# Scan of a hybrid RWKV-7 encoder on one core: b and k in one load, values by heads and tokens, systems in longer rows

## The chip, the core and the metric

The kernel runs on one NeuronCore of a Trainium2 chip. The core has a matrix engine (TensorE, PE in the profile, with its weight loads as PEld), a vector engine (VectorE, DVE), a scalar engine (ScalarE, ACT), a general engine (GpSimd, POOL) and a sync engine (SyncE, SP). In this kernel SP issues nearly all transfers between DRAM and on-chip memory (SBUF); ACT issues a few from its own queue (ACTq). All transfers run on the same 16 DMA engines, as packets. Matmul results land in PSUM and are copied out by ACT or DVE. The metric is the device time of one execution in microseconds (us), lower is better.

## The reference

The reference is an encoder of two layers over 256 prompt tokens and 1024 sample tokens of 1024 features: a bidirectional RWKV-7 mixer, a neighbourhood attention, and an MLP after each. The change touches only the RWKV-7 mixer, whose core is a linear recurrence, run per head (16 heads of 64 features) forward and backward:

```
def _wkv_scan(r, w, k, v, a, b, reverse):
    def step(S, inp):
        r_t, w_t, k_t, v_t, a_t, b_t = inp
        sa = jnp.einsum('bhvk,bhk->bhv', S, a_t)
        S = S * w_t[:, :, None, :] + sa[..., None] * b_t[:, :, None, :] + v_t[..., None] * k_t[:, :, None, :]
        return S, jnp.einsum('bhvk,bhk->bhv', S, r_t)
    ...
    _, y = lax.scan(step, s0, seq, reverse=reverse)
    return jnp.moveaxis(y, 0, 1)
```

## The kernel before

**Stages.** The projections of the first layer come first (up to about 690 us of the profiled run), then the scan (to about 1365 us), then output projection, MLP, attention and second MLP. All arithmetic is float32, the large matmuls as three passes over split operands.

**The scan in chunks.** The 1280 tokens are 20 chunks of 64 (4 of the prompt, 16 of the sample). Inside a chunk the recurrence is solved in closed form: for each head, chunk and direction a triangular system of 64 x 64 has to be inverted, after which the state is handed on by matmuls. Two heads lie in the upper and lower 64 partitions of a tile, so every product is issued as a pair of 64-row matmuls (`pair`, L976). There are ten jobs of 16 chunks with two directions: jobs 0 and 1 take the prompt (four head pairs of four chunks each), jobs 2 to 9 the sample of one head pair each. A job has eight groups `(d, g)`: direction d, four chunks.

**What a job does.** The preparation stage has stored, per head pair and direction, `ar_d` (a in columns 0 to 63, r in 64 to 127) and `bk_d` (b in columns 0 to 63, k in 64 to 127), and `v_block` has stored the values into `v_d`. Then, for each job:

- `load` (L801, L802) brings a group's `ar` (128 partitions x 4 x 128) and `bb`, the b half of `bk_d` (128 x 4 x 64). `prod` multiplies them into `aps`; ACT copies the system half into `zb` (L814), DVE masks the other (L815). `store` (L818) writes the systems to a DRAM scratch `dd`, one for each direction, laid out `[16 chunks, 2 heads, 64, 64]`.
- `mload` (L833) reads the diagonal blocks of 32 x 32 back, so that each partition holds one block: direction 0 into `mt`, direction 1 into `mraw`, two transfers each. Four ACT copies `mtr` (L842) turn `mraw` into the second half of `mt`. DVE inverts all 128 blocks together in 31 rank-one steps (L853, L855).
- `qst` stores the inverse `q` and its transpose `qt` (L866, L870) to scratch `qd`; `qld` (L886, L891) loads them as `qq` and `qx`; `merge1` and `merge2` join the blocks of 32 into inverses of 64 (`yps`, `qps`).
- `kload` (L917) loads all of `bk_d` for the group (128 x 4 x 128), about 30 time units after the b half of the same rows was loaded; `kprod`, `kmask` and `ktr` make `kps`, `zk`, `lps` and `lt` of it.
- `vload` (L954) loads the values: `v_d` is `[tokens, 1024]`, so a partition (a token of the chunk) gets rows of 64 floats (256 bytes). Jobs 0 and 1 need 16 such transfers of 64 KB, the others 4 of 256 KB.
- `scan_step` runs 16 steps in each direction (16 time units): matmuls into `wu` and `yo`, with ACT copies `up` (L997), `u` (L1011) and `S` (L1019) between them. `scan_post` normalises and stores the result.

**What sets the order.** Every piece has a due time in units of a step, `at(t, f)`; sorted by due time, the pieces give PE, DVE, ACT and POOL an order written out by hand, in which each engine runs strictly. SP's order is not written out this way; it issues in order too. The systems of a job are prepared about 34 units (two jobs) ahead. Tiles of `ar`, `bb` and `zb` come from rings (`nxt`): `bb` has four slots and `ar` and `zb` 20 each, ten of them in the pool `er` that is opened during the value projection (`scan_begin`) and ten in `rp`, opened when the scan begins (`scan`). `bk` has three buffers. A load into a ring waits until the readers of the slot's last content are done.

**Around it.** `v_block` projects the values in 40 blocks of 128 tokens x 256 features (L510 to L512); ACT copies the result to `vt` (two buffers) and issues the store itself (L517). `gate_begin` loads the gate's operands during the last job through `graw`, of seven buffers.

Of the kernel before, what the change touches and what calls it, by code (L numbers as in the profile page):

```python
# [5 lines left out]
F32 = mybir.dt.float32  # L6
# [7 lines left out]
P = 128  # L14
T = 1280
# [3 lines left out]
L = 64  # L19
# [29 lines left out]
class Trunk:  # L49
# [50 lines left out]
    def l0_proj(self):  # L100
# [2 lines left out]
        r_d = self.dram("r_d", [2, P, T])  # L103
        vm_d = self.dram("vm_d", [8, P, T])
        sg_d = self.dram("sg_d", [160, T])
        v_d = self.dram("v_d", [T, 1024])
        pos = [1, 258, 770]
        W = 1283

# [296 lines left out]
        ev = {}  # L406
# [41 lines left out]
        def vmm(i):  # L448
            q, tb = i // 10, i % 10
            vw = [tuple(z[:, k % 2 * 256:k % 2 * 256 + 256] for z in wq["v", q, k // 2]) for k in range(KT)]  # L450
            ev[i] = self.v_block(act, vw, v_d, (vp, "vt", 256, 2), (self.pa, "aps"), q, tb, later=True)
        for i in range(40):
            at(vt(i), vmm, i)
            at(vt(i) + VL, lambda i=i: ev.pop(i)())
# [45 lines left out]
            self.v_split(vp, self.v_raw(w, vp, q, g), out, 8, str(q % 2), self.nc.vector)  # L500
        return out

    def v_block(self, act, vw, dst, tp, pp, q, tb, scale=1.0, later=False):

        nc = self.nc
        ps = pp[0].tile([P, 512], F32, name="vps", tag=pp[1])
        ts_ = slice(tb * P, (tb + 1) * P)
        for k in range(KT):
            ah, al = act[k]
            nc.tensor.matmul(ps[:, :256], ah[:, ts_], vw[k][0], start=k == 0, stop=False)  # L510
            nc.tensor.matmul(ps[:, :256], ah[:, ts_], vw[k][1], start=False, stop=False)  # L511
            nc.tensor.matmul(ps[:, :256], al[:, ts_], vw[k][0], start=False, stop=k == KT - 1)  # L512

        def evac():
            vt = tp[0].tile([P, tp[2]], F32, name="vt", tag=tp[1], bufs=tp[3])
            nc.scalar.activation(vt[:, :256], ps[:, :256], AF.Copy, scale=scale)
            nc.scalar.dma_start(dst[ts_, q * 256:(q + 1) * 256], vt[:, :256])  # L517
        if later:
            return evac
        evac()  # L520
# [183 lines left out]
    def scan_begin(self):  # L704

        nc, tc = self.nc, self.tc
        self.dram("z_d", [8, P, T])
        self.spool = lambda name, bufs, **kw: self.sctx.enter_context(tc.tile_pool(name=name, bufs=bufs, reuse_waits="tile", **kw))


        self.ectx = ExitStack()
        er = self.er = self.ectx.enter_context(tc.tile_pool(name="er", bufs=1, reuse_waits="tile", side="right"))
        self.r_bb, self.r_ar, self.r_zb = ([[er.tile([P, 4, w], F32, name=f"{name}{i}") for i in range(n)], 0] for name, n, w in
                                           (("bb", 4, L), ("ar", 10, P), ("zb", 10, P)))
        self.dsc = self.sctx.enter_context(tc.tile_pool(name="dsc", bufs=4, space=DRAM))
# [16 lines left out]
    def scan(self):  # L732
# [9 lines left out]
        self.lnx = fx.tile([P, 8, 2, L], F32, name="lnx")  # L742
        for e in range(2):
            nc.sync.dma_start(self.lnx[self.half(1 - e)], self.a["lnx"][:, :, 64 * e:64 * e + 64].unsqueeze(0).to_broadcast([64, 8, 2, L]))
        grow(self.r_ar, rp, "ar", [P, 4, P], 10)
        grow(self.r_zb, rp, "zb", [P, 4, P], 10)
        self.sp = pool("sp", 4)
        self.yp = pool("yp", 2)
        self.pa = self.pt = self.sctx.enter_context(tc.tile_pool(name="pa", bufs=4, space=PSUM, reuse_waits="tile"))
# [30 lines left out]
    def scan_job(self, j):  # L780
# [8 lines left out]
        T0 = -34.0  # L789

        def first(J=J):
            J["dd"] = [self.dsc.tile([16, 2, 64, 64], F32, name="dd", tag="dd") for _ in range(2)]
        at(T0, first, min(j + 1, 3))
        for n, (d, g) in enumerate(order):
            m, c0 = grp[g]
            t = T0 + 2 * n
            E = 1 if j == 0 else 2 if j == 1 and n < 2 else 3

            def load(d=d, g=g, m=m, c0=c0):
                ar, bb = self.nxt(self.r_ar), self.nxt(self.r_bb)  # L800
                nc.sync.dma_start(ar, self.ar_d[m, d, :, c0:c0 + 4, :])  # L801
                nc.sync.dma_start(bb, self.bk_d[m, d, :, c0:c0 + 4, 0:64])  # L802
                J["ar"][d, g], J["bb", d, g] = ar, bb

            def prod(c, d=d, g=g):
                ar, bb = J["ar"][d, g], J["bb", d, g]
                if c == 0:
                    J["zb"][d, g] = self.nxt(self.r_zb)
                    J["pa"] = self.pa.tile([P, 4, P], F32, name="aps", tag="aps")
                ps = J["pa"]  # L810
                if c < 4:
                    self.pair(lambda e, z: (ps[z, c, :], bb[z, c, :], ar[z, c, :]))
                if c == 4:
                    nc.scalar.copy(J["zb"][d, g][:, :, 0:64], ps[:, :, 0:64])  # L814
                    nc.vector.tensor_tensor(out=J["zb"][d, g][:, :, 64:128], in0=ps[:, :, 64:128], in1=self.mask[d][:, 64:128].unsqueeze(1).to_broadcast([P, 4, L]), op=ALU.mult)  # L815

            def store(d=d, g=g, j=j):
                nc.sync.dma_start(J["dd"][d].rearrange("c e s t -> (e s) c t")[:, 4 * g:4 * g + 4, :], J["zb"][d, g][:, :, 0:64])  # L818
            at(t - (1.614 if j else 7.0), load, E)
            for c in range(5):  # L820
                at(t + (c * 0.133 + -0.013 if c < 4 else 0.577), lambda c=c, f=prod: f(c), E)
            at(t + (1.263 if j else 1.011), store, E)
# [4 lines left out]
        def mload():  # L827
            mt = self.er.tile([P, 32, 32], F32, name="mt", tag="mt")
            raw = self.er.tile([P, 32, 32], F32, name="mraw", tag="mraw")
            for d in range(2):  # L830
                for b in range(2):
                    o, bs = 64 * d + 32 * b, slice(32 * b, 32 * b + 32)
                    nc.sync.dma_start((mt, raw)[d][o:o + 32], J["dd"][d].rearrange("c e s t -> (c e) s t")[:, bs, bs])  # L833
# [40 lines left out]
        def qld():  # L874
            Q = self.nxt(self.r_q)
            qx = [self.nxt(r) for r in self.r_qx]
            J["Q"], J["qx"] = Q, qx
            for d in range(2):
                hi = 32 - 32 * d
                nc.gpsimd.memset(Q[:, :, d, hi:hi + 32], 0.0)  # L880
            for d in range(2):
                for b in range(2):
                    o = 64 * d + 32 * b
                    for e in range(2):
                        q0 = 64 * e + 32 * b
                        nc.sync.dma_start(Q[q0:q0 + 32, :, d, 32 * b:32 * b + 32], J["qd"][d, o:o + 32].rearrange("(c e) s t -> e s c t", e=2)[e])  # L886

                o = 96 * d
                for e in range(2):
                    r0 = 64 * e + 32 * d  # L890
                    nc.sync.dma_start(qx[d][r0:r0 + 32], J["qd"][1 - d, o:o + 32].rearrange("(c e) s t -> e s c t", e=2)[e])  # L891
        at(T3 + 0.807, qld)

        for n, (d, g) in enumerate(order):
# [17 lines left out]
            at(t + 0.52, merge1)  # L912
            at(t + 1.30, merge2)

            def kload(d=d, g=g, m=m, c0=c0):
                bk = J["bk", d, g] = self.rp.tile([P, 4, P], F32, name="bk", tag="bk", bufs=3)
                nc.sync.dma_start(bk, self.bk_d[m, d, :, c0:c0 + 4, :])  # L917
# [12 lines left out]
            def ktr(c, d=d, g=g):  # L930
# [9 lines left out]
            at(t - 1.9, kload)  # L940
# [5 lines left out]
        def vload():  # L946
# [1 line left out]
            vd = self.scr["v_d"]  # L948
            parts = [(grp[0][0], grp[0][1], 0, 16)] if grp[0][1] else [(m, c0, 4 * g, 4) for g, (m, c0) in enumerate(grp)]
            for m, c0, k, n in parts:  # L950
                rows = slice(c0 * L, (c0 + n) * L)
                for i in range(2):
                    for e in range(2):
                        nc.sync.dma_start(vt[self.half(e ^ i), i, k:k + n], vd[rows, m * P + 64 * e:m * P + 64 * e + 64].rearrange("(c s) v -> s c v", s=L))  # L954
        at(-5.423, vload)

        def yalloc():
# [225 lines left out]
    def gate_begin(self):  # L1183
# [5 lines left out]
        def begin():  # L1189
# [6 lines left out]
            gp.tile([P, 512], F32, name="graw", tag="graw", bufs=7)  # L1196
            self.wo = []

        def load(src, c0, c1, stacked):
            raw = self.gp.tile([P, 512], F32, name="graw", tag="graw", bufs=7)  # L1200
            raw = raw[:, :c1 - c0]
            if stacked:
                for j in range(3):
# [696 lines left out]
```

## Time and profile before

| What | Value |
|---|---|
| median of 3 timed runs | 4072.04 us (4071.78 to 4072.08) |
| the profiled execution's own time | 4061.69 us |
| its span | 4059.9 us |
| PE busy | 3818.0 us (94%) |
| DVE busy | 2244.7 us (55%) |
| ACT busy | 1580.4 us (39%) |
| POOL busy | 1339.0 us (33%) |
| DMA packets | 450885, 394.89 MB; 267456 of them under 512 bytes |

The profile is that of one execution. Busy time counts compute instructions; issuing a transfer is listed by queue (SPq, ACTq). A row of the waits names an engine, the instruction that waited, what it waited for, then the total in us, how often, and the longest. A row of the timeline gives start, length, engine, line, operation, tiles, count, and in brackets the idle time before it and what ended it. "issue" is idle time of an engine that waited for nothing that the profile shows.

### The profile page before, as it was taken

The page shows a single profiled execution, that of the slowest core. Times are in us where ns is not written, and L with a number is a line of the kernel's source. Part 1 is how long each engine was busy: PE and PEld are TensorE (multiplying, and loading weights), DVE is VectorE, ACT ScalarE, POOL GpSimd, SP SyncE. Part 2 cuts the span into 40 slices and gives each one's busy share as a digit, 9 for nine tenths or more (in the row PEclk, how much of TensorE's full clock was granted, in tenths as well). Part 3 has the DMA queues.
Part 4 walks back from the last instruction along what each step waited for, and adds up shares of the span by engine and source line. Part 5 has one row for each costly group of instructions (what it writes and reads, how often), then busy time and mean ns, then how long its engine had stood idle before and what let it go on. Part 6 is the DMA issues. An engine that isn't in the chain of part 4 may idle for free.

```text
span 4059.9 us, 91014 instructions
## 1 busy us (share of the span) xinstructions
PE 3818.0 (94%) x36820; PEld 3225.7 (79%) x36820; DVE 2244.7 (55%) x4581; ACT 1580.4 (39%) x3868; POOL 1339.0 (33%) x1252
## 2 busy tenths in 40 slices
PE   8989988788888799999999999999989999999999
PEld 5765578787888688888888879887778888888888
DVE  5777742466565547555555562355554755555555
ACT  6776642455555431111111133466563211111111
POOL 4446542022122434222222241344443422222222
PEclk9987889899999899999999999999999999999999
DMA  4236564767664430111111115344464110111101
GB/s 142 71 102 223 194 216 121 163 159 169 157 158 122 131 113 32 42 38 36 42 37 37 42 51 168 113 111 108 94 181 150 40 41 33 42 37 37 42 32 63
DMA packets 450885, 394.89 MB, mean 97 GB/s; under 512 B 267456, under 2 KB 352832, under 8 KB 450464
## 3 DMA queue, kind: packets, MB, share of 16 engines
q1 hardware_dynamic: 416048, 327.72, 28.5%
q10 hardware_dynamic: 34416, 61.35, 4.2%
q8 instruction: 289, 4.73, 0.5%
q14 instruction: 132, 1.08, 0.1%
HBM read 270.50 MB, written 124.44 MB: 97 GB/s over the span
## 4 chain that ended last, share of the span: by engine, by line
PE 78%; DVE 6%; ACT 5%; DMA 4%; issue 3%; POOL 3%; SPq 1%; ACTq 0%; DVEq 0%; POOLq 0%
PE ps L95 19%; PE ps L96 18%; PE ps L97 18%; PE wu L976 4%; PE vps L510 1%; PE vps L512 1%; PE vps L511 1%; PE kps L976 1%; PE aps L976 1%; PE lps L976 1%; PE op L1815 1%; PE yo L976 1%; PE pt L1758 1%; PE yps L976 1%; DMA dd<-zb 1%
## 5 line engine op out<-in xcount | busy, mean ns | idle before, releaser
L1361 DVE TENSOR_TENSOR x<-ps,x 128x256 f32<-128x256 f32 x1488 | 814.1, 594 | 644.9 <-PE ps L97 644.8
L95 PE MATMUL ps<-ah,whi 128*128 128x512 f32 (+1 forms) x2304 | 842.4, 366 | 0.0
L96 PE MATMUL ps<-al,whi 128*128 128x512 f32 (+1 forms) x2304 | 825.8, 358 | 0.0
L97 PE MATMUL ps<-ah,wlo 128*128 128x512 f32 (+1 forms) x2304 | 823.1, 357 | 1.8 <-DVE wlo L90 1.5
L90 POOL TENSOR_TENSOR wlo<-raw,whi 128x1024 fp32r<-128x1024 f32 (+1 forms) x178 | 390.5, 2194 | 850.5 <-ACT whi L89 826.2
L95 PE MATMUL ps<-hh,whi 128*128 128x512 f32 (+1 forms) x1536 | 547.1, 356 | 9.4 <-DVE x L1361 9.4
L96 PE MATMUL ps<-hl,whi 128*128 128x512 f32 (+1 forms) x1536 | 546.3, 356 | 0.0
L97 PE MATMUL ps<-hh,wlo 128*128 128x512 f32 (+1 forms) x1536 | 545.8, 355 | 0.0
L95 PEld LDWEIGHTS ps<-ah,whi 128*128 128x128 f32 x2304 | 434.4, 189 | 72.2 <-issue 7.8
L97 PEld LDWEIGHTS ps<-ah,wlo 128*128 128x128 f32 x2304 | 433.4, 188 | 72.3 <-DVE wlo L90 1.9
L96 PEld LDWEIGHTS ps<-al,whi 128*128 128x128 f32 x2304 | 434.5, 189 | 62.5 <-issue 1.0
L89 ACT CAST whi<-raw 128x1024 fp32r<-128x1024 f32 (+1 forms) x206 | 200.3, 972 | 709.1 <-PE ps L96 624.9
L1340 POOL TENSOR_TENSOR rl<-rl 128x512 f32<-128x512 f32 (+1 forms) x192 | 173.7, 905 | 506.0 <-PE ps L97 462.5
L95 PEld LDWEIGHTS ps<-hh,whi 128*128 128x128 f32 x1536 | 291.2, 190 | 53.8 <-DVE x L1361 11.4
L97 PEld LDWEIGHTS ps<-hh,wlo 128*128 128x128 f32 x1536 | 291.4, 190 | 41.7
L96 PEld LDWEIGHTS ps<-hl,whi 128*128 128x128 f32 x1536 | 291.0, 189 | 40.7
L1339 ACT ACTIVATE rl<-ps 128x512 f32<-128x512 f32 (+1 forms) x192 | 100.7, 525 | 555.9 <-PE ps L97 555.9
L1342 ACT CAST hh<-rl 128x512 fp32r<-128x512 f32 (+1 forms) x192 | 105.6, 550 | 323.6 <-POOL rl L1340 323.6
L1343 DVE TENSOR_TENSOR hl<-rl,hh 128x512 fp32r<-128x512 f32 (+1 forms) x192 | 119.7, 624 | 143.1 <-ACT hh L1342 142.7
L1752 POOL TENSOR_TENSOR s<-s,mx 128x384 f32<-128x384 f32 (+1 forms) x150 | 109.7, 744 | 163.6 <-DVE mx L1751 115.4
L1057 POOL TENSOR_TENSOR y<-y,mu 128x512 f32<-128x512 f32 x18 | 19.3, 1073 | 370.4 <-DVE mu L1054 370.4
L853 DVE TENSOR_TENSOR tmp<-mt,q 128x31 f32<-128x31 f32 (+15 forms) x310 | 114.0, 368 | 43.3 <-ACT mt L842 20.3
(302 smaller groups left out, 8270.1 us busy)
## 6 DMA issues: line engine op xcount, KB each, us to landing
raw<-in_w_down_dram SPq DMA_DIRECT2D x64, 512.0 KB
raw<-in_w_up_dram SPq DMA_DIRECT2D x64, 512.0 KB
ar<-ar_d SPq DMA_DIRECT2D x80, 256.0 KB
bk<-bk_d SPq DMA_DIRECT2D x80, 256.0 KB
ar_d<-ar ACTq DMA_DIRECT2D x32, 512.0 KB
bk_d<-bk ACTq DMA_DIRECT2D x32, 512.0 KB
bs<-tab SPq DMA_DIRECT2D x128, 96.0 KB
v_d<-vt ACTq DMA_DIRECT2D x80, 128.0 KB
```

The costliest lines, as they stand in the source:

```text
L89: nc.scalar.copy(hi[:, cs], raw)
L90: lo_eng.tensor_tensor(out=lo[:, cs], in0=raw, in1=hi[:, cs].bitcast(F32), op=ALU.subtract)
L95: mm(ps, sh, mh, start=first, stop=False)
L96: mm(ps, sh, ml, start=False, stop=False)
L97: mm(ps, sl, mh, start=False, stop=last)
L853: nc.vector.tensor_tensor(out=tv, in0=mt[:, 0:jj, jj:jj + 1].to_broadcast([P, jj, w]), in1=q[:, jj:jj + 1, jj:].to_broadcast([P, jj, w]), ...
L976: self.nc.tensor.matmul(out, w, x, start=start, stop=stop, skip_group_check=free)
L1340: nc.gpsimd.tensor_tensor(out=r[:, :n], in0=r[:, :n], in1=r[:, :n], op=ALU.mult)
L1342: nc.scalar.copy(hh[:, :n], r[:, :n])
L1343: nc.vector.tensor_tensor(out=hl[:, :n], in0=r[:, :n], in1=hh[:, :n].bitcast(F32), op=ALU.subtract)
L1361: nc.vector.tensor_tensor(out=xv, in0=ps[:, :n], in1=xv, op=ALU.add)
L1752: nc.gpsimd.tensor_tensor(out=s[:, :nk], in0=s[:, :nk], in1=mx[:, 2:3].to_broadcast([P, nk]), op=ALU.mult)
```

## The change

- **b and k in one load.** `load` fetches the whole of `bk_d` for the group (128 x 4 x 128) with `ar`, and the tile is kept until `ktr`. `bb`, its ring and `kload` go. `bk` gets a ring of 20, and the rings of `ar`, `zb` and `bk` have twelve slots in `er` and eight in `rp`. `graw` has six buffers instead of seven.
- **Values by heads and tokens.** `v_d` becomes `[16 heads, 64 tokens of a chunk, 20 chunks, 64]`. A block of values, which holds two chunks, is stored by two transfers of 64 partitions instead of one of 128, in rows of 256 bytes; a load reads, per partition, one row of 4 x 64 floats (jobs 0, 1) or 16 x 64 floats (the others).
- **Systems in longer rows.** `dd` becomes `[128, 16, 64]`: a group's store writes one row of 1 KB per partition instead of four of 256 bytes at four places. `mload` reads each block of 32 partitions in two transfers, one per head, with rows of 128 bytes that lie 4 KB apart along the block's row; `qld` reads with heads before chunks accordingly.

The due times of what stays are the same. The computation is the same.

```
-            nc.scalar.dma_start(dst[ts_, q * 256:(q + 1) * 256], vt[:, :256])
+            if heads:
+                for i in range(2):
+                    nc.scalar.dma_start(dst[4 * q:4 * q + 4, :, 2 * tb + i].rearrange("h s v -> s h v"), vt[64 * i:64 * i + 64, :256].rearrange("s (h v) -> s h v", v=L))
+                return
...
-        self.r_bb, self.r_ar, self.r_zb = ([[er.tile([P, 4, w], F32, name=f"{name}{i}") for i in range(n)], 0] for name, n, w in
-                                           (("bb", 4, L), ("ar", 10, P), ("zb", 10, P)))
+        self.r_bk, self.r_ar, self.r_zb = ([[er.tile([P, 4, P], F32, name=f"{name}{i}") for i in range(12)], 0] for name in ("bk", "ar", "zb"))
...
-            J["dd"] = [self.dsc.tile([16, 2, 64, 64], F32, name="dd", tag="dd") for _ in range(2)]
+            J["dd"] = [self.dsc.tile([P, 16, 64], F32, name="dd", tag="dd") for _ in range(2)]
...
-                nc.sync.dma_start(bb, self.bk_d[m, d, :, c0:c0 + 4, 0:64])
+                nc.sync.dma_start(bk, self.bk_d[m, d, :, c0:c0 + 4, :])
...
-                nc.sync.dma_start(J["dd"][d].rearrange("c e s t -> (e s) c t")[:, 4 * g:4 * g + 4, :], J["zb"][d, g][:, :, 0:64])
+                nc.sync.dma_start(J["dd"][d][:, 4 * g:4 * g + 4], J["zb"][d, g][:, :, 0:64])
...
-                    nc.sync.dma_start((mt, raw)[d][o:o + 32], J["dd"][d].rearrange("c e s t -> (c e) s t")[:, bs, bs])
+                    for e in range(2):
+                        nc.sync.dma_start((mt, raw)[d][o + 16 * e:o + 16 * e + 16], J["dd"][d][64 * e + 32 * b:64 * e + 32 * b + 32, :, bs].rearrange("s c t -> c s t"))
...
-            def kload(d=d, g=g, m=m, c0=c0):
-                bk = J["bk", d, g] = self.rp.tile([P, 4, P], F32, name="bk", tag="bk", bufs=3)
-                nc.sync.dma_start(bk, self.bk_d[m, d, :, c0:c0 + 4, :])
...
-                        nc.sync.dma_start(vt[self.half(e ^ i), i, k:k + n], vd[rows, m * P + 64 * e:m * P + 64 * e + 64].rearrange("(c s) v -> s c v", s=L))
+                        nc.sync.dma_start(vt[self.half(e ^ i), i, k:k + n], vd[2 * m + e, :, c0:c0 + n])
```

More of the change, by code (lines that the diff above doesn't have):

```diff
@@ L105, in l0_proj @@
         sg_d = self.dram("sg_d", [160, T])
-        v_d = self.dram("v_d", [T, 1024])
+        v_d = self.dram("v_d", [16, L, 20, L])
         pos = [1, 258, 770]
@@ L450, in vmm @@
             vw = [tuple(z[:, k % 2 * 256:k % 2 * 256 + 256] for z in wq["v", q, k // 2]) for k in range(KT)]
-            ev[i] = self.v_block(act, vw, v_d, (vp, "vt", 256, 2), (self.pa, "aps"), q, tb, later=True)
+            ev[i] = self.v_block(act, vw, v_d, (vp, "vt", 256, 2), (self.pa, "aps"), q, tb, later=True, heads=True)
         for i in range(40):
@@ L501, in v_weights, with v_block @@
         return out
-    def v_block(self, act, vw, dst, tp, pp, q, tb, scale=1.0, later=False):
+    def v_block(self, act, vw, dst, tp, pp, q, tb, scale=1.0, later=False, heads=False):
         nc = self.nc
@@ L744, in scan @@
             nc.sync.dma_start(self.lnx[self.half(1 - e)], self.a["lnx"][:, :, 64 * e:64 * e + 64].unsqueeze(0).to_broadcast([64, 8, 2, L]))
-        grow(self.r_ar, rp, "ar", [P, 4, P], 10)
-        grow(self.r_zb, rp, "zb", [P, 4, P], 10)
+        grow(self.r_bk, rp, "bk", [P, 4, P], 8)
+        grow(self.r_ar, rp, "ar", [P, 4, P], 8)
+        grow(self.r_zb, rp, "zb", [P, 4, P], 8)
         self.sp = pool("sp", 4)
@@ L799, in load @@
             def load(d=d, g=g, m=m, c0=c0):
-                ar, bb = self.nxt(self.r_ar), self.nxt(self.r_bb)
+                ar, bk = self.nxt(self.r_ar), self.nxt(self.r_bk)
                 nc.sync.dma_start(ar, self.ar_d[m, d, :, c0:c0 + 4, :])
-                nc.sync.dma_start(bb, self.bk_d[m, d, :, c0:c0 + 4, 0:64])
-                J["ar"][d, g], J["bb", d, g] = ar, bb
+                nc.sync.dma_start(bk, self.bk_d[m, d, :, c0:c0 + 4, :])
+                J["ar"][d, g], J["bk", d, g] = ar, bk
             def prod(c, d=d, g=g):
-                ar, bb = J["ar"][d, g], J["bb", d, g]
+                ar, bk = J["ar"][d, g], J["bk", d, g]
                 if c == 0:
@@ L811, in prod @@
                 if c < 4:
-                    self.pair(lambda e, z: (ps[z, c, :], bb[z, c, :], ar[z, c, :]))
+                    self.pair(lambda e, z: (ps[z, c, :], bk[z, c, 0:64], ar[z, c, :]))
                 if c == 4:
@@ L885, in qld @@
                         q0 = 64 * e + 32 * b
-                        nc.sync.dma_start(Q[q0:q0 + 32, :, d, 32 * b:32 * b + 32], J["qd"][d, o:o + 32].rearrange("(c e) s t -> e s c t", e=2)[e])
+                        nc.sync.dma_start(Q[q0:q0 + 32, :, d, 32 * b:32 * b + 32], J["qd"][d, o:o + 32].rearrange("(e c) s t -> e s c t", e=2)[e])
                 o = 96 * d
@@ L890, in qld @@
                     r0 = 64 * e + 32 * d
-                    nc.sync.dma_start(qx[d][r0:r0 + 32], J["qd"][1 - d, o:o + 32].rearrange("(c e) s t -> e s c t", e=2)[e])
+                    nc.sync.dma_start(qx[d][r0:r0 + 32], J["qd"][1 - d, o:o + 32].rearrange("(e c) s t -> e s c t", e=2)[e])
         at(T3 + 0.807, qld)
@@ L939, in ktr @@
                     nc.scalar.copy(lt, ps)
-            at(t - 1.9, kload)
             at(t + 1.25, kmask)
@@ L950, in vload @@
             for m, c0, k, n in parts:
-                rows = slice(c0 * L, (c0 + n) * L)
                 for i in range(2):
                     for e in range(2):
-                        nc.sync.dma_start(vt[self.half(e ^ i), i, k:k + n], vd[rows, m * P + 64 * e:m * P + 64 * e + 64].rearrange("(c s) v -> s c v", s=L))
+                        nc.sync.dma_start(vt[self.half(e ^ i), i, k:k + n], vd[2 * m + e, :, c0:c0 + n])
         at(-5.423, vload)
@@ L1195, in begin @@
             self.gate = [[gp.tile([P if i < 2 else 96, n], F32R, name=nm + "hls"[i]) for i in range(3)] for nm, n in (("sg", T), ("g", 1024))]
-            gp.tile([P, 512], F32, name="graw", tag="graw", bufs=7)
+            gp.tile([P, 512], F32, name="graw", tag="graw", bufs=6)
             self.wo = []
         def load(src, c0, c1, stacked):
-            raw = self.gp.tile([P, 512], F32, name="graw", tag="graw", bufs=7)
+            raw = self.gp.tile([P, 512], F32, name="graw", tag="graw", bufs=6)
             raw = raw[:, :c1 - c0]
```

## The prediction

> **What bounds the kernel now.** I first read, by stretch, the engines' busy time together with the DMA share (columns: stretch, length, PE, PEld, DVE, ACT, POOL, granted clock, DMA share, GB/s): start of the scan, its middle, its last job but one.
>
> ```profile
> core 0 of [0], span 4059.9 us
> 683.00:740.00 57.00, 29.71 (x412) 27.64 (x411) 13.40 (x40) 11.91 (x28) 11.24 (x23) 0.76 0.77 183
> 740.00:1257.00 517.00, 454.41 (x15104) 422.33 (x15100) 309.86 (x792) 299.69 (x1121) 114.24 (x135) 0.98 0.66 159
> 1257.00:1315.00 58.00, 51.36 (x1812) 47.81 (x1810) 35.30 (x85) 32.18 (x129) 14.24 (x16) 0.98 0.42 109
> ```
>
> PE is busy for 454 of 517 us in the middle, 88%, while the DMA engines are busy for 0.66 of the time. So the middle is PE's, and transfers count only through PE's 63 idle us. The start is different: PE idles for 57 - 29.7 = 27 us there. In the next-to-last job DMA falls to 0.42, but PE is still 89% busy: most of PE's idle time isn't bought by transfers. How long a job is comes from the `u` copies, 32 to a job (times in ns, then first and last start):
>
> ```profile
> L1011 ACT COPY u<-wu x257: 193/212/240, 740.1 to 1256.8; 128x64 f32<-128x64 f32 x129
> ```
>
> Eight jobs in 1256.8 - 740.1 = 517 us are 64.6 us each. Then PE's own waits in the middle (total us, times, longest), and, below, the rows of that kind in the next-to-last job:
>
> ```profile
> PE wu L976 <- issue: 8.9, 16, 1.5
> PE lps L976 <- issue: 7.8, 11, 2.0
> PE qps L976 <- issue: 4.1, 5, 1.6
> PE yo L976 <- issue: 3.9, 7, 1.1
> PE aps L976 <- issue: 3.6, 4, 1.9
> PE aps L976 <- DMA ar<-ar_d: 2.1, 1, 2.1
> PE yps L976 <- issue: 1.7, 4, 0.6
> PE kps L976 <- issue: 1.7, 3, 0.8
> PE zps L976 <- issue: 1.2, 3, 0.8
> ```
>
> ```profile
> PE kps L976 <- issue: 0.9, 2, 0.5
> PE lps L976 <- issue: 0.6, 2, 0.3
> ```
>
> The visible wait for a data transfer is 2.1 us in eight jobs. The rows that end in "issue" add up to 32.9 us: PE waits for nothing that the profile shows. Their likeliest cause is PE's own instructions, which arrive as packets on a DMA queue, 118 in the middle and 15 in the next-to-last job:
>
> ```profile
> q8 instruction: 118, 1.93, 1.6%
> q8 instruction: 15, 0.25, 1.7%
> ```
>
> Idle "issue" per instruction packet is 32.9 / 118 = 0.279 us at a DMA share of 0.66, and 1.5 / 15 = 0.10 us at 0.42.
>
> **The change part by part.**
>
> *The packets that go.* Two narrow stretches of the value projection give prices: the first (3.5 us) holds almost only 256-byte packets (0.34 MB in 1361), the second (10 us) almost only value stores in rows of 1 KB (three stores are 384, the rest of its packets partial stores and completions):
>
> ```profile
> q1 hardware_dynamic: 1361, 0.34, 42.8%
> q10 hardware_dynamic: 576, 0.52, 15.1%
> ```
>
> A 256-byte packet takes 0.428 x 16 x 3.5 / 1361 = 17.6 ns; a KB in long rows at most 0.151 x 16 x 10 / 520 KB = 46 ns. A `bb` load is 512 packets, so 512 x 17.6 / 16 = 0.56 us of all engines, and eight go from each job: 4.5 us. A job's values are 4 x 1024 packets, 4.5 us, and become 1 MB in rows of 4 KB, at most 1024 x 46 / 16 = 2.9 us: 1.6 us less. The `dd` stores I take as unchanged, because the SBUF side still has pieces of 256 bytes; if packets grow to 1 KB it is 8 x (0.56 - 128 x 46 / 16000) = 1.5 us more. `mload`'s and `qld`'s packets stay at 128 bytes. So 6.1 of 64.6 us go, and the DMA share falls by 0.094 to about 0.57. If the idle time per instruction packet falls in a line with the share, (0.279 - 0.10) / (0.66 - 0.42) = 0.75 us per unit, it is 0.094 x 0.75 x 118 = **8 us less**. The ends are nothing (the idle time has another cause) and 0.179 x 118 = 21 us (all that the quiet job lacks). I take the line, since both of its ends are measured.
>
> [...]
>
> *The start of the scan.* SP's and PE's timelines, in order of queue:
>
> ```profile
> 684.31 0.36 SPq L802 DMA_DIRECT2D bb<-bk_d  x1
> 695.84 0.32 SPq L870 DMA_DIRECT2D qd<-qt  x1
> 702.84 0.38 SPq L802 DMA_DIRECT2D bb<-bk_d  x1
> 705.83 0.37 SPq L818 DMA_DIRECT2D dd<-zb  x1
> 706.25 10.48 SPq L954 DMA_DIRECT2D v<-v_d  x16
> 703.43 5.55 PE L976 MATMUL aps<-ar,bb 64*64 64x128 f32 x48 [9.45 <-DMA ar<-ar_d]
> 721.32 1.39 PE L976 MATMUL yps<-qx,zb 64*64 64x32 f32 x15 [12.34 <-DMA qx<-qd]
> 729.57 1.65 PE L976 MATMUL aps<-ar,bb 64*64 64x128 f32 x16 [2.65 <-DMA bb<-bk_d]
> 736.55 0.33 PE L976 MATMUL aps<-ar,bb 64*64 64x128 f32 x2 [1.29 <-DMA bb<-bk_d]
> ```
>
> The first inverse is stored at 695.84; PE can't merge until `qx` has landed, and SP issues 16 value loads, 10.48 us, ahead of it. Issue times, in ns (least, median, most):
>
> ```profile
> L954 SPq DMA_DIRECT2D v<-v_d x64: 579/586/1257, 706.3 to 1270.1; - x64
> L917 SPq DMA_DIRECT2D bk<-bk_d x80: 319/382/1750, 701.8 to 1334.2; - x80
> L833 SPq DMA_DIRECT2D mraw<-dd x20: 321/565/1952, 646.3 to 1245.8; - x20
> ```
>
> The new value load has, like `bk`, one row for each partition, so 382 for 586: 16 x 0.204 = 3.3 us. Ends: nothing, if 64 partitions set the price, and 16 x 0.267 = 4.3 by the least. Ahead of that SP stands from 703.22 (702.84 + 0.38) to 705.83, 2.6 us, for a `dd` store whose product ran late, after an `ar` load that came late (9.45). The queue's own waits say why:
>
> ```profile
> SPq L802 <- PE aps L976: 21.6, 1, 21.6
> ```
>
> SP stood for 21.6 us, up to the `bb` load at 684.31, which waited for one of four slots. With twelve slots in `er` that wait is gone, and slots 10 and 11 of `ar` need no memory of `rp`. What is late next is `rp`, which frees when the value projection ends; so I take the 2.6 us, and half of the 3.9 us (2.65 + 1.29) in which PE waits for `bb` behind the values: 2. That loads now bring 256 KB where `bb` brought 128 stands against it; `kload`'s issues in this stretch go. Sum 3.3 + 2.6 + 2 = 7.9; less two more `mraw` issues ahead of job 1's inverse (2 x 0.565 = 1.1): **7 us less**. Ends: 4 more (nothing gained, and four `mload` issues and the larger loads paid), and 12.3 + 3.9 = 16 less.
>
> *What is added.* Each of 40 value blocks gets a second store on ACT's queue:
>
> ```profile
> L517 ACTq DMA_DIRECT2D v_d<-vt x37: 326/327/691, 566.8 to 691.7; - x37
> 663.35 0.38 ACT L516 ACTIVATE vt<-vps 128x256 f32<-128x256 f32 x1 [2.50 <-PE vps L512]
> ```
>
> It costs 0.33, or, as three-dimensional as the old value load, up to 0.59 + 0.26 us a block; ACT idles 2.50 us a block from 600 on, and PE hides it. The first ten blocks lie among the preparation's work; there up to 10 x 0.85 us could show. Behind a waiting `vt` stand, on ACT, the copies of the preparation, and PE waits for those. I take 1 us, since the 2.50 us row is the nearest. Job 0's products now need ten loads of 256 KB instead of 128 KB, 1.3 MB more ahead of weight loads on the same queue; at 159 GB/s that is 8 us of transfer, with PE busy on blocks already cut. I take 1 us. **Together 2 us more**, ends 0 and 8.5 + 8 = 16.
>
> *Costed at nothing.* Two more loads for each direction in `mload`: direction 0's hide in the flight of the last `dd` store (3.62 us below). SP loses eight `bb` issues a job and gains four of `mload`. The fuller rings: `bk` lives 34 units, a slot comes round after 20 loads at 2 units, 40. `graw` with six reuses a slot 3.6 units after its load's due time, past the cut at 2.
>
> *Sum.* -8 - 7 + 2 = -13 us; the profiled execution's 4061.69 (span 4059.9 and 1.8 around it) becomes 4048.7. The timed median lies 10.35 us above the profiled run, a difference between launches that I carry over: 4072.0 - 13 = **4059**.
>
> **The rivals.**
>
> *The transfers were hidden anyway.* PE's "issue" time has another cause than the traffic, such as the products of later jobs, which the quiet job lacks. For it: only 2.1 us of visible data waits. Against it: a job has as many instruction packets as the quiet one (118 / 8 = 14.8, and 15), yet more idle time for each. [...] Then only the start is left, -7 + 2: 4067; with a start that only shifts its wait, 4072.
>
> *The inverse comes late.* The chain of waits has these pieces, once a job:
>
> ```profile
> 785.52 3.62 DMA dd<-zb
> 789.66 4.40 DMA mraw<-dd
> 719.01 2.17 DMA qx<-qd
> ```
>
> And what the copies of `mraw` sat idle for (us, times), over the whole scan:
>
> ```profile
>   DMA mraw<-dd: 9.1, 6
> ```
>
> ACT already waits for `mraw` in six of ten jobs, 9.1 us in all, and behind that copy in ACT's fixed order stand `S`, `u` and `up`, for which PE waits. The second direction's four issues instead of two land 1.1 us later, and rows 4 KB apart might be read at half the speed, 4.4 us. In the eight jobs where PE is full, 8 x (1.1 + 4.4) = 44 us: 4103. It decides from 13 / 8 = 1.6 us of lateness a job (no gain left), and 2.6 us make it slower than 0.2%. Against it: `qx`, also rows of 128 bytes read with steps of KBs, lands in 2.17 us. [...]
>
> *More than I think.* If all of the quiet job's difference and most of the start come: -21 - 13 + 2: 4040. That `dd` isn't written in longer packets at all, only in longer rows, is my forecast's case; longer ones would add 1.5 / 64.6 x 0.75 x 118 = 2 us.
>
> **How the numbers follow.** A measurement of this kernel tells about 0.2%, 8.1 us, from no change: faster is below 4063.9, slower above 4080.2. Forecast (8 to 25 us less) 0.46; more than that 0.08; hidden anyway 0.30; inverse late or the value stores' costs in full 0.16. So faster 0.54, same 0.30, slower 0.16. The range runs from 4038 (a little under the third rival's 4040) to 4082, where nothing is gained and 10 of the 16 us of added costs, or as much lateness, are paid; more of these, about 0.1, and greater gains, about 0.1, stay outside.
>
> **What would show it.** In the changed profile: no `bb`, 80 loads of `bk` at the place of `ar`; a DMA share near 0.57 in the middle; "issue" rows near 25 us for 118 instruction packets; value loads issued in about 0.38 us, and `yps` waiting for `qx` some 6 us less; no 21.6 us wait of SP at the start. Wrong it would be with an unchanged job length of 64.6 us, with `mt` waiting for `mraw` by more than 1.6 us a job, or with PE waiting for `vt` before 600 us.

## The result, and the profile after

| What | Before | After |
|---|---|---|
| median of the timed runs (8 each, side by side) | 4070.2 us (4063.15 to 4082.34) | 4087.4 us (from 4079.86) |
| ratio, 95% interval | 1 | **1.0038 [1.0026, 1.0050]** |
| span of the profiled execution | 4059.9 us | 4078.3 us |

The changed kernel is slower by 0.38%, some 15.5 us (0.0038 x 4070); 13 us less had been forecast. One of its eight runs was disturbed (10530 us) and is not part of the ratio.

**Some of the forecast rows came.** The middle of the scan in the profile after, with the columns of the first fence of the prediction, and the line of the page on packets:

```profile
740.00:1257.00 517.00, 452.23 (x14836) 422.50 (x14834) 303.25 (x780) 294.35 (x1094) 106.93 (x126) 0.96 0.58 143
```

```profile
DMA packets 388420, 384.40 MB, mean 94 GB/s; under 512 B 206016, under 2 KB 288320, under 8 KB 388000
```

62465 packets are gone, the DMA share of the middle is 0.58 (forecast 0.57). PE's largest waits in that stretch (total us, times, longest):

```profile
PE wu L975 <- ACT S L1018: 15.2, 7, 3.4
PE wu L975 <- ACT u L1010: 7.9, 13, 1.0
PE yo L975 <- ACT u L1010: 7.9, 8, 1.4
PE yo L975 <- issue: 7.4, 10, 1.6
PE aps L975 <- ACT mt L847: 4.1, 1, 4.1
PE wu L975 <- issue: 3.7, 6, 0.9
PE aps L975 <- issue: 3.7, 4, 2.3
```

All rows that end in "issue" add up to 19.5 us, where 32.9 had been and 25 were forecast. But the rows in which PE waits for another engine add up to 39.7 us, 16.7 more than the 23.0 of before. The largest was a small one before:

```profile
PE wu L976 <- ACT S L1019: 3.1, 5, 1.0
```

Three of the forecast rows did not come: `yps` waited 10.60 us for `qx`, 1.74 less than before and not 6; job 0's value loads took 0.594 us each and not 0.38; and SP still stood for more than 20 us at the start. Of the signs of being wrong, two came: the copies of `mraw` waited 15.6 us in eight jobs, 1.95 us a job and more than the 1.6 named, and the jobs did not become shorter (65.8 us, read from the `u` copies as before, for 64.6). PE's wait for `vt` before 600 us stayed what it had been (5.6 us, before 5.8).

**Why ACT's S is late.** What the copies of `mraw` waited for in the middle, before and then after:

```profile
ACT mt L842 <- DMA mraw<-dd: 3.4, 4, 1.3
```

```profile
ACT mt L847 <- DMA mraw<-dd: 15.6, 7, 3.5
ACT mt L847 <- DMA dd<-zb: 3.4, 1, 3.4
```

ACT waits 19.0 us for the reload of the systems instead of 3.4. One job in order of time, SP and then ACT, before (start, length, engine, line, what; idle time before it in brackets):

```profile
785.52 1.11 SPq L818 DMA_DIRECT2D dd<-zb  x1
787.52 1.00 SPq L833 DMA_DIRECT2D mt<-dd  x2
789.16 1.15 SPq L833 DMA_DIRECT2D mraw<-dd  x2
794.16 0.62 ACT L842 COPY mt<-mraw 64x256 f32<-64x256 f32 x1 [1.09 <-DMA mraw<-dd]
```

and after, one job later:

```profile
861.27 0.39 SPq L822 DMA_DIRECT2D dd<-zb  x1
862.29 2.03 SPq L838 DMA_DIRECT2D mt<-dd  x4
864.36 4.13 SPq L838 DMA_DIRECT2D mraw<-dd  x4
871.02 0.63 ACT L847 COPY mt<-mraw 64x256 f32<-64x256 f32 x1 [1.64 <-DMA mraw<-dd]
871.67 0.31 ACT L1018 ACTIVATE S<-wu,dall 128x64 f32<-128x64 f32 x1
872.03 0.27 PE L975 MATMUL wu<-S,ar 64*64 64x64 f32 x2 [1.48 <-ACT S L1018]
```

Read downwards: direction 0's issues do run in the flight of the last store, as the prediction had it. Direction 1's four follow, with nothing of SP's queue among them, and take 4.13 us where two had taken 1.15: not every issue costs the same, and two of the four are longer than the other two (1.19 and 1.84 us, beside 0.49 and 0.48). From the last store's issue to ACT's first copy it is 871.02 - 861.27 = 9.75 us, before 8.64. S stands behind the copy in ACT's order, and PE behind S. Read in the same way for jobs 2 to 9, direction 1's issues take 1.15 us before and 3.13 after (medians), and the median distance from the last store to the copy is 9.08 us before and 10.14 after.

**What the stall costs beside itself.** The same stretch of the profile after by the clock (the last three columns are granted clock, DMA share, GB/s):

```profile
870.00:872.03 2.03, 0.56 (x24) 0.42 (x20) 0.36 (x1) 0.96 (x3) 1.95 (x3) 1.00 0.33 82
872.03:874.00 1.97, 0.95 (x28) 0.81 (x32) 0.00 (x0) 1.90 (x5) 1.68 (x2) 0.96 0.74 220
874.00:877.30 3.30, 3.12 (x60) 2.93 (x62) 1.37 (x5) 1.58 (x5) 0.00 (x0) 0.51 0.94 281
877.30:880.00 2.70, 2.65 (x90) 2.41 (x86) 2.19 (x9) 1.52 (x7) 0.00 (x0) 1.00 0.96 238
```

PE is idle for some 2.5 of 4 us, and then has half its clock for 3.3 us, in which it does 60 matmuls; in the 2.7 us after that it does 90. The kernel before has such stretches too (0.51 from 798.40 to 801.70 us, behind the copy of the job shown above); after the change more of the time passes in them. Over the middle the granted clock is 0.96 for 0.98, and a matmul takes 452.23 / 14836 = 30.5 ns for 30.1: 14836 x 0.4 = 6 us.

**Where the profiled execution became longer.** The copies of the value blocks and the `u` copies mark the stages (count, ns, first and last start), before and after:

```profile
L516 ACT ACTIVATE vt<-vps x40: 373/383/392, 545.7 to 691.2; 128x256 f32<-128x256 f32 x40
L1011 ACT COPY u<-wu x320: 193/212/240, 740.1 to 1364.9; 128x64 f32<-128x64 f32 x160
```

```profile
L516 ACT ACTIVATE vt<-vps x40: 373/384/392, 548.5 to 702.7; 128x256 f32<-128x256 f32 x40
L1010 ACT COPY u<-wu x320: 194/213/254, 749.3 to 1381.9; 128x64 f32<-128x64 f32 x160
```

The value projection (first to last `vt`) took 154.2 us for 145.5, 8.7 more; from there to the first `u` 46.6 for 48.9, 2.3 less; the scan (first to last `u`) 632.6 for 624.8, 7.8 more. With 2.8 us before the first `vt` and 1.4 behind the last `u` these are the 18.4 us between the spans. So there are two losses: one in the scan, where 13.4 us of "issue" went and more came back as waits for ACT and a lower clock, and one in the value projection.

### The profile page after: what moved, and what is told of

It reads as the page before. It is cut to its first block, busy times and chain, and to the rows that moved or that the text cites. A ratio compares the mean times of both kernels' runs of the same rounds, so it can differ in the third digit from the quotient of the medians.

```text
span 4078.3 us, 90867 instructions
## 1 busy us (share of the span) xinstructions
PE 3831.4 (94%) x36820; PEld 3239.6 (79%) x36820; DVE 2246.5 (55%) x4581; ACT 1581.2 (39%) x3868; POOL 1340.2 (33%) x1252
## 4 chain that ended last, share of the span: by engine, by line
PE 75%; DVE 7%; DMA 5%; ACT 5%; issue 3%; POOL 2%; SPq 2%; ACTq 0%; DVEq 0%; POOLq 0%
PE ps L95 18%; PE ps L96 18%; PE ps L97 18%; PE wu L975 4%; PE vps L510 1%; PE vps L511 1%; PE vps L512 1%; PE kps L975 1%; PE op L1814 1%; PE aps L975 1%; SPq L838 1%; PE pt L1757 1%; PE lps L975 1%; DVE q L860 1%; DMA mraw<-dd 1%
## 5 line engine op out<-in xcount | busy, mean ns | idle before, releaser
L95 PEld LDWEIGHTS ps<-hh,whi 128*128 128x128 f32 x1536 | 291.2, 190 | 53.8 <-DVE x L1360 11.4
```

The costliest lines, as they stand in the source:

```text
L95: mm(ps, sh, mh, start=first, stop=False)
```

## The experiments

The executions of one kernel differ by up to 26 us, so the verdicts rest on the ratios (five rounds each, against runs of before on the same chip), and the traces, of one execution each, say where to look. Line numbers shift a little between kernels. The expectations name their theories by letters and say what each means; three go through the later ones. W: the reload lands later, and whoever waits for it in a fixed order holds PE up. L: the order heads before chunks in `qld` costs. Q: more issues hold up SP's queue and what is loaded behind them.

**One part alone (e1 to e3).** Each is the kernel before with one of the three parts of the diff that is shown above: e1 with `v_d` by heads and tokens, e2 with the new `dd`, `mload` and `qld`, e3 with the whole of `bk_d` in `load` and no `kload`.

> The kernel before with the value layout alone (two stores of 64 partitions per block, loads with one row per partition). Theory A (the value stores are what costs: two issues of about 0.62 us on ACT's queue instead of one of 0.33, and blocks that wait for them): 8 to 14 us slower than before, the 40th value block 8 to 12 us later. Rival B (job 0's larger loads crowd the stores, the layout itself costs little): within 3 us of before. Rival C (the inverse's reload costs): within 3 us, or up to 4 us faster by the cheaper value loads at the start of the scan.

> The kernel before with the layout of the systems alone (stores in rows of 1 KB, reload in eight transfers instead of four, inverses loaded by heads). Theory A: within 3 us of before. Rival B: within 3 us. Rival C (the reload of the blocks lands later and ACT, in its fixed order, stands at its copy): 6 to 12 us slower, ACT's waits for the reloaded blocks near 24 us in total instead of 9.

> The kernel before with b and k in one load alone (rings of 20, no second load). Theory A: 4 to 12 us faster than before, since only the gain of the change is left. Rival B (256 KB instead of 128 KB per load ahead of the value stores and weights): 4 to 10 us slower, with the 40th value block 5 to 10 us later. Rival C: 4 to 12 us faster.

**Two parts (e4, e5).** The changed kernel without the value layout, and without the systems layout.

> The changed kernel without its value layout. Theory A: 2 to 10 us faster than before, 12 to 25 us faster than the changed kernel. Rival B: 4 to 10 us slower than before. Rival C: 2 to 8 us slower than before, most of the changed kernel's loss kept.

> The changed kernel without its layout of the systems (stores and reload of the systems as before). Theory D (the layout of the systems is the whole of the loss): 8 to 18 us faster than the kernel before, 25 us or more faster than the changed kernel. Rival E (the value stores cost too once loads of 256 KB run beside them): between 4 us faster and 6 us slower than before.

Measured:

| Kernel | b and k | systems | values | ratio | 95% interval |
|---|---|---|---|---|---|
| e1 | | | x | 0.9997 | 0.9987 to 1.0007 |
| e2 | | x | | 1.0043 | 1.0029 to 1.0057 |
| e3 | x | | | 0.9961 | 0.9947 to 0.9975 |
| e4 | x | x | | 1.0017 | 1.0005 to 1.0029 |
| e5 | x | | x | 0.9984 | 0.9973 to 0.9994 |
| after | x | x | x | 1.0038 | 1.0026 to 1.0050 |

One part gains: b and k in one load, 0.39%, 16 us. The systems cost 0.43% alone, 0.56% with b and k (e4 against e3) and 0.54% with both others (after against e5). The values cost nothing alone, but 0.23% and 0.21% where b and k are loaded whole (e5 against e3, after against e4); by the intervals each of these two differences is uncertain by some 0.17%. So theory A fell with e1, rival B with e3, and e2 and e4 went rival C's way, e2 with more than its 6 to 12 us. e5 lies between its two theories. In the trace of e3 the value projection and the scan are both shorter than before (141.1 and 621.4 us):

```profile
L516 ACT ACTIVATE vt<-vps x40: 370/384/391, 548.9 to 690.0; 128x256 f32<-128x256 f32 x40
L1006 ACT COPY u<-wu x320: 194/213/244, 735.7 to 1357.1; 128x64 f32<-128x64 f32 x160
```

The two spans differ by only 4.1 us, because the profiled execution of before lay below its median by more than that of e3 did. So the traces do not show where all of the 16 us lie.

With the values added to it (e5) the projection took 149.9 us:

```profile
L516 ACT ACTIVATE vt<-vps x40: 373/383/393, 549.8 to 699.7; 128x256 f32<-128x256 f32 x40
L519 ACTq DMA_DIRECT2D v_d<-vt x80: 581/623/1422, 550.2 to 700.7; - x80
```

In the four profiled kernels that have all three parts (after, e9, e10, e13) it took 152.7 to 156.8 us. There are 80 stores of 0.62 us, where 40 of 0.33 had been, so a block's stores take 1.25 us of ACT's queue. That this delay costs only with the larger loads beside it is what the ratios suggest; which transfer holds which was not taken apart.

**What in the systems costs (e6, e7, e8, e11).** The part changes the layout of `dd`, the number of reload transfers and the order heads before chunks. e6 keeps the old `dd` and only splits the reload in eight, by head:

```
-  nc.sync.dma_start((mt, raw)[d][o:o + 32], J["dd"][d].rearrange("c e s t -> (c e) s t")[:, bs, bs])
+  for e in range(2):
+      nc.sync.dma_start((mt, raw)[d][o + 16 * e:o + 16 * e + 16], J["dd"][d][:, e, bs, bs])
```

> The kernel before, its systems stored as before, but the reload of each block split by head into two transfers (eight a job instead of four), into 16 partitions each. Theory F (the number of reload transfers costs: the last is issued 2 us later, ACT stands at its copy): 8 to 18 us slower than before, ACT's waits for the reloaded blocks 18 to 27 us. Rival G (rows of 128 bytes that lie 4 KB apart are read slowly): within 4 us of before, waits near 9 us.

Measured 1.0049 [1.0031, 1.0066]: the split costs as much as the whole part. e7 is e2 with a row of 4352 bytes instead of 4096 in `dd`, so that the rows a partition reads no longer lie 4 KB apart:

> The layout of the systems alone, its rows padded from 4096 to 4352 bytes, still eight reload transfers. Theory F: as the layout without padding, 12 to 22 us slower than before. [...]

Measured 1.0054 [1.0038, 1.0070]: a step of exactly 4 KB is not the cause. e8 lays `dd` out as [64, 32, 64], so that four transfers reload it, and stores each group in two transfers instead:

> The kernel before with systems laid out by row, then head and chunk (step of 8192 bytes between the rows of a block), so that four transfers reload a job; each group is stored by two transfers of 64 partitions with rows of 1 KB instead of one. Theory F: within 6 us of before, ACT's waits for the reloaded blocks 5 to 14 us. Rival G: 10 us or more slower, waits above 20 us.

Measured 1.0061 [1.0045, 1.0077]: theory F, which asked for 6 us at most, missed. Three things differ from before in e8: the stores ahead of the reload are doubled (eight more issues a job), the rows of a block lie 8 KB apart, and `qld` has the new order. ACT's wait for `mraw` is 10.6 us in the middle, so rival G's waits above 20 us did not come either. Which of the three costs was not taken apart. e6, e7 and e8 all had the new order in `qld`. e11 is e6 without it (a transfer goes to every second partition):

```
+  for e in range(2):
+      nc.sync.dma_start((mt, raw)[d][o + e:o + 32:2], J["dd"][d][:, e, bs, bs])
```

> The kernel before, reload in eight transfers by head as in e6, but with the order chunks before heads kept in mt, q and qld (a transfer goes to every second partition). It differs from before in the count of transfers alone. Theory W: ratio 1.003 to 1.005, ACT's waits for mraw 18 us or more. Theory L: 0.999 to 1.001, since qld is that of before.

Measured 1.0043 [1.0030, 1.0057]. e11 differs from before in eight transfers for four, with the same bytes and rows, and in the partitions that one transfer goes to; e6, whose transfers go to neighbouring partitions, lost as much. The split alone has the whole loss. Theory L is out.

**The wait moved in the written order (e9, e10, e12).** e9 is the changed kernel with ACT's copies and the inversion 0.4 units later, e12 the kernel before with both 0.4 units earlier (from job 1 on):

```
-  at(T1 + 0.912 + 0.14 * i, lambda i=i: mtr(i), 1 if j == 0 else 3)
+  at(T1 + (0.912 + 0.4 if j else 0.912) + 0.14 * i, lambda i=i: mtr(i), 1 if j == 0 else 3)
...
-  T2 = T1 + (1.63 if j else 2.359)
+  T2 = T1 + (1.63 + 0.4 if j else 2.359)
```

> The changed kernel; from job 1 on the four copies of mraw and the inversion behind them stand 0.4 units (about 1.6 us) later in the written order; every transfer as in the changed kernel. Theory W (the reload lands some 2 us later in eight issues, ACT waits for it in its fixed order, and PE, which then waits for S, goes on at half clock): ACT's waits for mraw fall from 23.6 us to 12 or less, PE's wait of wu for S goes to 5 or less, ratio to before 0.996 to 1.000. Theory L (the order heads before chunks in qld, with 4 KB instead of 8 KB between the rows it reads, costs, not the wait of ACT): ratio stays 1.003 to 1.005 although the waits fall. If the inverse has no 1.6 us to spare behind it, waits of yps for qx appear instead, and the ratio stays above 1.002.

> The kernel before with every transfer unchanged; from job 1 on the copies of mraw and the inversion stand 0.4 units (about 1.6 us) earlier in the written order, so that the unchanged reload is late for them. Theory W: ACT's waits for mraw rise from 9.1 to 20 us or more, ratio 1.003 to 1.006. Theory L: within 0.001 of 1.

e9 measured 1.0056 [1.0044, 1.0068], slower still. PE's waits in its middle:

```profile
PE wu L975 <- ACT up L996: 21.3, 21, 3.7
PE wu L975 <- DVE zk L929: 18.9, 15, 3.0
...
PE wu L975 <- ACT S L1018: 0.6, 2, 0.4
```

The wait for S went (0.6 us), as theory W had it, but its ratio of 0.996 to 1.000 did not come: the copies now stood ahead of `up`, and DVE's inversion ahead of `zk`, and PE waited for those. PE also waited 12.0 us for `bk` and `ar` and 3.0 us for `qx`. e12 measured 1.0007 [0.9998, 1.0017], where theory W asked for 1.003 to 1.006; its copies came earlier in the order, but in most jobs ACT came to them no sooner than the reload: its wait for `mraw` grew to 5.0 us in the middle only. It failed to make the reload late. PE's wait for S grew all the same, in many short pieces:

```profile
PE wu L976 <- ACT S L1019: 11.0, 20, 1.1
```

e11 has nearly the same total in 6 waits (11.4 us), at a granted clock of 0.96 where e12 has 0.98. So the total of this wait in a trace is not yet a loss. e10 is the changed kernel with direction 1's four transfers ahead of direction 0's (`for d in (1, 0)` in `mload`):

> The changed kernel, with the four transfers of direction 1 (mraw, which ACT waits for) issued ahead of the four of direction 0 (mt, which only DVE needs, 0.7 units later). Theory W with SP's issues as the cause of the lateness: the last mraw transfer is issued up to 2 us sooner, ACT's waits for mraw fall from 23.6 to 12 us or less, ratio 0.997 to 1.001. If the direction 0 transfers were issued in the flight of the last store anyway and the last store is what comes late, nothing is gained: 1.003 to 1.005. Theory L: 1.003 to 1.005.

Measured 1.0027 [1.0014, 1.0040], with ACT waiting 14.5 us in the middle: direction 1's systems are stored last, so its transfers wait for that store either way. What e10 gains on the changed kernel (1.0038) is within the intervals.

**The copies taken off ACT (e13, e14).** POOL makes them, at the same due times; e13 is the changed kernel so, e14 is e3 so:

```
-  nc.scalar.copy(J["mt"][64:128, ts, :], J["raw"][64:128, :, ts].rearrange("p s t -> p t s"))
+  nc.gpsimd.tensor_copy(J["mt"][64:128, ts, :], J["raw"][64:128, :, ts].rearrange("p s t -> p t s"))
```

> The changed kernel with the four copies of mraw to mt made by POOL instead of ACT, at the same due times; all transfers as in the changed kernel. Theory W: ACT has no wait for mraw, PE's wait of wu for S falls from 15.2 to 5 us or less, ratio to before 0.995 to 1.000. Theory Q (four more issues of SP hold up the loads behind them): 1.003 to 1.005 as before. If POOL, behind DVE's means in its own order, comes late with the copies, DVE's first product of the inverse waits for POOL and yps for qx: above 1.002 with those rows.

> The part with b and k in one load alone, with the copies of mraw made by POOL. Theory W: ACT's remaining 9.9 us of waits for mraw go (6.8 of them in the eight jobs in which PE is full or less), so 0.993 to 0.996. Theory Q: 0.995 to 0.997, as without the edit.

e13: 1.0007 [0.9997, 1.0016], 0.31% better than the changed kernel, though less than theory W asked for (0.995 to 1.000). e14, as theory W had it: **0.9941 [0.9929, 0.9953]**, 4054.0 us beside 4078.3: the best kernel of this study, faster than both. PE's wait for S is nearly gone in e13 (1.6 us), but DVE's first product of the inverse now waits for POOL, in e13 and in e14:

```profile
DVE tmp L858 <- POOL mt L847: 30.9, 7, 5.5
```

```profile
DVE tmp L853 <- POOL mt L842: 14.5, 7, 2.8
```

The late reload is still late. It only meets DVE's order instead of ACT's, twice as long with eight transfers as with four; `zk`, for which PE waits 18.7 us in e13 and 13.9 in e14, stands behind that product.

**Issues added to the kernel before (e15 to e18).** Four more transfers a job, into a tile that nobody reads, stand ahead of the reload transfers (one before each) or behind them all; 64 KB each in e15 and e16, 4 KB in e17 and e18:

```
+  nc.sync.dma_start(dum[o:o + 16], J["dd"][d][:, 0, bs, bs])
   nc.sync.dma_start((mt, raw)[d][o:o + 32], J["dd"][d].rearrange("c e s t -> (c e) s t")[:, bs, bs])
```

```
+  nc.sync.dma_start(dum[o:o + 16, 0:2], J["dd"][d][:, 0, 32 * b:32 * b + 2, bs])
   nc.sync.dma_start((mt, raw)[d][o:o + 32], J["dd"][d].rearrange("c e s t -> (c e) s t")[:, bs, bs])
```

> The kernel before, with four more transfers a job on SP, each half a reload transfer into a tile that nobody reads, one ahead of each of the four reload transfers: the reload is late by four issues (about 2 us) as in the changed kernel, in its old shape. Theory W: 1.003 to 1.006, ACT's waits for mraw 18 us or more. Theory Q: 1.003 to 1.006.

> The same four more transfers, all behind the four reload transfers: the reload is not late, what SP issues behind it is. Theory W: 0.999 to 1.0015, ACT's waits for mraw near 9 us. Theory Q: 1.003 to 1.006.

> The kernel before, with four more transfers a job of 4 KB each (32 packets of 128 bytes) into a tile that nobody reads, one ahead of each reload transfer. Theory W (the reload comes late for whoever waits for it in a fixed order): 1.003 to 1.006, ACT's waits for mraw 18 us or more. Theory Q (four more issues hold up SP's queue): 1.003 to 1.006. If only the packets counted: 0.999 to 1.0015.

> The same four small transfers behind the four reload transfers. Theory W: 0.999 to 1.0015, ACT's waits for mraw near 9 us. Theory Q: 1.003 to 1.006. If only the packets of e16 counted: 0.999 to 1.0015.

| Kernel | ratio | 95% interval | last store to ACT's copy, median of jobs 2 to 9 | ACT's wait for `mraw`, middle |
|---|---|---|---|---|
| e15, 64 KB ahead | 1.0102 | 1.0088 to 1.0117 | 13.97 us | 43.2 us |
| e16, 64 KB behind | 1.0044 | 1.0030 to 1.0057 | 10.25 us | 7.0 us |
| e17, 4 KB ahead | 1.0007 | 0.9997 to 1.0018 | 10.44 us | 13.0 us |
| e18, 4 KB behind | 1.0011 | 1.0001 to 1.0021 | 9.49 us | 3.5 us |

e15 and e16 issue the same transfers in another order, and the order alone makes 0.58%: ACT's copy starts 3.7 us later, and in e15 PE waits for S as never before:

```profile
PE wu L978 <- ACT S L1021: 33.5, 9, 6.5
```

So a late reload costs. e16 itself is a miss for theory W, which asked for 1.0015 at most. e18 shows that four more issues on SP, with little to move, cost about 0.1% (theory Q is out as the cause of 0.4%), and e16 against e18 that 1920 packets a job more (2048 of 128 bytes for 128) cost 0.3%. e17 is a miss too: four small issues ahead of the reload should have cost as much as the split, and cost nothing that can be told from e18. Its trace shows the copies 1.35 us late (10.43 for 9.08) and PE's wait for S at 10.3 us, but it is that of the slowest of its eleven runs (4090 us beside a median of 4080), and the others left none.

**All traces side by side.** In the middle of the scan, for the kernels whose written order is that of before, sums in us:

| Kernels | DMA share | "issue" | ACT for `mraw` | PE for S |
|---|---|---|---|---|
| four reload transfers, nothing added ahead: before, e1, e3, e5, e16, e18 | 0.58 to 0.68 | 28.3 to 46.9 | 2.1 to 8.2 | 2.7 to 6.2 |
| eight: after, e2, e4, e6, e7, e10, e11 | 0.57 to 0.66 | 19.5 to 35.6 | 11.1 to 18.2 | 10.5 to 16.4 |

The groups don't overlap in the last two columns. Of the kernels in neither row with ACT's copies in their old place, e8 has 10.6 and 10.4 us there, e15 43.2 and 33.5, e17 13.0 and 10.3. From the last store to the end of the last issue into `mraw` it is 5.6 to 6.2 us (median of jobs 2 to 9) in the first row and 7.0 to 8.2 in the second. From the last store to the copy it is 9.1 to 10.3 us and 10.1 to 11.1: there the rows touch, since e16, with more to move, has 10.25.

## Why the prediction was wrong, point by point

**"Costed at nothing": the two more loads for each direction in `mload`.** This is the step that failed. It said that direction 0's hide in the flight of the last store, which they do, and left direction 1's out of the sum. Only the rival "the inverse comes late" counted them, at 1.1 us a job, with 0.16 for that rival and the value stores together. Measured, direction 1's issues take 2.0 us more (3.13 for 1.15), and the copies start 1.06 us later in the changed kernel (10.14 for 9.08). The split alone costs 0.43%, 17.5 us (e11, and e2 as much); with b and k loaded whole the systems cost 0.54 to 0.56%, some 22 us. By the ratios the change is -16 us for b and k, +22 for the systems and +9 for the values, +15 in all; the sum had nothing for the second but 1.1 us at the start. The sign was already in the profile: ACT waited for `mraw` in six of ten jobs, and PE behind it for S. The prediction read "the visible wait for a data transfer is 2.1 us" from PE's own rows, where a wait for a transfer that comes by way of ACT has ACT's name. A step that adds to a wait that already ends last can't be costed at nothing.

**The price of lateness.** The rival reckoned one us lost for each us of lateness: 8 x 1.1 = 9 us without its slow rows. No one price comes out of the runs: the copies start 1.79 us later in e2 and 1.60 in e11 (14 and 13 us in eight jobs) for 17.5 us each, and 1.35 us later in e17's one trace, with no loss that can be told. The traces have one part of what comes on top: the granted clock is lower (0.96 for 0.98), which makes 6 us in the changed kernel. The rival's other half, rows 4 KB apart read at half the speed, was an assumption that no run shows, and it is not needed: e11 has the whole loss of e2 without such rows.

**The packets that go.** The rows came out in kind and size. Forecast: share 0.57, "issue" 25 us. Over the eight kernels with b and k in one load the share is 0.57 to 0.59 and the "issue" rows average 25.8 us; over the twelve without it 0.64 to 0.68 and 35.4 us. The difference is 9.6 us, for 8 forecast. Without the kernels that load a tile nobody reads, or move work in the written order or to POOL, it is 6.7 us (26.5 and 33.2). Single traces scatter widely about it (12.5 to 31.2, and 27.9 to 46.9), so the line through two stretches of one trace was lucky in its precision. That these us are what e3 gains was not shown. The idle time follows the traffic, and e16's packets cost 0.3%, but that it is the fetch of instructions that waits was not tested.

**The start of the scan.** Mis-sized: 7 us forecast, 2.3 measured between the last `vt` and the first `u` (3.2 in e3). The 16 value loads of job 0 took 0.594 us each where 0.382 was taken from `bk`, 0.614 before:

```profile
L953 SPq DMA_DIRECT2D v<-v_d x16: 487/594/596, 714.5 to 726.6; - x16
```

They have 64 partitions and rows of 1 KB; the row of `bk` was not the nearest, the old value load itself was. And SP's stall of 21.6 us did not go:

```profile
SPq L818 <- ACT zb L814: 22.6, 2, 22.0
```

That is e3, up to 700 us: the wait moved from the `bb` load to the store behind it, which waits for ACT's copy of the systems. In the changed kernel SP issues nothing from 663.4 to 696.1 us, where that copy ends (of these, its rows put 22.5 us down to a value store and 10.1 to the copy). "What is late next" was asked, and answered with the pool instead of the next piece of the queue.

**What is added.** Forecast 2 us for the value stores and job 0's loads, with 0 and 16 as ends. Alone the stores cost nothing (e1), with the larger loads 0.21 to 0.23%, 9 us. The ends held, the value was too low. It was the sum of two costs taken apart; by the ratios the stores cost only where the larger loads are.

**The rivals' chances.** "The transfers were hidden anyway" has e3 against it: 16 us gained, more than the 13 of the whole forecast and the 5 that this rival left, though the traces do not show where they lie. "The inverse comes late" and the projection's 9 us decided the result, at 1.06 us of lateness a job, below that rival's own limit of 1.6. The two had been given 0.16 together.

**What stays open.** Shown is that the split in eight alone costs 0.43% (e11), that a reload made late by order alone costs (e15 against e16), and that with the split ACT, or DVE in its place, waits longer for it (all traces). Not shown is that lateness makes up all of the 0.43%: e17 issued as many transfers ahead of the last reload as e11 and lost nothing that can be told, and in e12 PE waited 11.0 us for S at 1.0007. The copies off ACT did not bring all of it back either, as the wait went on to DVE. A kernel in which nobody waits for the reload in a fixed order was not tried. How larger loads and value stores meet in the projection was not taken apart.

## What to carry to other kernels

Where the profile shows an engine already waiting for a transfer, however few us in all, don't cost a split of that transfer at nothing: it cost 0.4 to 0.6% here, more than fewer packets brought back. The count of issues alone is no measure of it (four small ones ahead, e17, cost nothing that could be told: 1.0007). Make a change's parts separable and time each: one part of three held all the gain, and alone, with a waiting copy moved to an idler engine, it made 0.9941 where the whole made 1.0038. When a wait is taken away, look for the next piece in the same queue before counting the gain.

## What the runs showed of the hardware that was not expected

PE's granted clock halved here behind short gaps: in the changed kernel PE was busy for 1.5 of the 4 us from 870 to 874, its waits there were 1.48 us for S and 1.02 us for `u`, and the next 3.3 us ran at 0.51. In the kernel before, the stretch at 0.51 from 798.40 us came behind waits of 0.99, 1.01 and 0.44 us. What brings the lower clock about was not tested.

The same 128 x 256 block costs ACT's queue 0.33 us to store in one transfer of 128 partitions and 2 x 0.62 us in two of 64 whose rows are also split by head (e5). The split of the reload by head costs too: 0.43% (e11).
